# A two-block transformer kernel whose program order comes from another timing model

## The chip, the cores and the metric

The kernel runs on one core of one Trainium2 chip. The metric is the device time of one execution in microseconds (us). The kernel before took a median of 1812.11 us over three runs, from 1811.02 to 1816.88.

## The reference, cut to what matters

256 tokens of 1024 features pass through a first block of two layers and then a second block of two layers. All arithmetic is float32.

A layer of the first block projects the tokens with one wide matrix and runs three attention-like branches: retention (4 heads in chunks of 128 tokens), sliding-window attention (6 heads) and latent attention (6 heads, keys and values expanded from a normalised latent). Their outputs are joined, projected and added to the scaled input, and a layer norm follows. Then a router picks for every token the best of 4 groups and two of the 4 experts in it, and 16 experts (gate and up projection, SiLU, down projection) are applied:

```python
mix = jnp.concatenate([ret_o, swa_o, mla_o], axis=-1) @ w_out[l]
x = layer_norm(DEEPNORM_ALPHA * x + mix, ln1_g[l], ln1_b[l])
ffn = grouped_moe(x, router_w, router_bias, exp_w_gate_up[l], exp_w_down[l])
x = layer_norm(DEEPNORM_ALPHA * x + ffn, ln2_g[l], ln2_b[l])
```

A layer of the second block is a feed-forward network with 2816 inner features, a mixer (windowed attention with 8 heads, pooling over four widths, and sigmoid gates on both branches) and a second such feed-forward network, each behind an RMS norm.

## The kernel before

**Weights.** All weights lie in DRAM in the order of use. `Weights.fill` (line 335) loads the next tile of up to 2048 columns by 128 rows on SyncE's queue into one of six buffers. `Weights._run` (line 342) takes the tiles apart into pieces of at most 1024 columns and splits each into two parts whose sum is the weight: ScalarE casts the high part (`whi`, line 358), and VectorE, or GpSimd for pieces listed by hand in `POOL_STEPS`, subtracts to get the low part (`wlo`, line 360). Five pieces can be open at a time:

```python
nc.scalar.copy(hi[:, :n], r[:, c : c + n])
engine = nc.gpsimd if (p is t[-1] and name == "dn") or self.step in self.pool_steps() else nc.vector
ins = engine.tensor_tensor(
    out=lo[:, :n], in0=r[:, c : c + n], in1=hi[:, :n].bitcast(F32), op=ALU.subtract
)
```

The activations are split in the same way, and every large product is three products (high by high, high by low, low by high), all issued from line 425.

**Stages.** `attention1` (line 647) makes the projections of the latents (`oq`, `okv`), retention's queries and keys (`orq`), values (`ov`), the expanded latents (`oqr`, `ouq`, `ouk`, `omv`), then latent attention through `attend` (line 770), the sliding-window projection (`osq`), retention (`og`, `scr`, `oret`), sliding-window attention and the output projection (`oo`). In `attend` the scores of a head (`sc`) go through `softmax_head` (line 600) on VectorE and ScalarE, are transposed (`pt`) and multiplied with the values (`po`). `moe` (line 1008) does the norm, the router (`lg`, `cn`), gathers the tokens by group (`og`) and runs the 16 experts (`ogu`, `yg`, `ya`). `ffn` (line 1266) runs 22 steps of 128 inner features (`u`, `v`, then the down projection `f` of the step before). At its head `rms_T` (line 532) transposes the tokens (`trx`, line 527), splits them (`xT`, lines 510 and 511) and takes the reciprocal root of the mean square (lines 492 to 501). `mixer` (line 1312) does queries and keys (`oq`), values (`ovp`), attention, pooling (`opl`), gates (`ogt`), branches (`obr`) and the output projection (`oz`), and ends with the sum `hmx` (line 1441):

```python
for t in range(2):
    for n in range(2):
        c = slice(n * 512, (n + 1) * 512)
        V.tensor_tensor(out=hn[:, t, c], in0=h[:, t, c], in1=oo[t][n], op=ALU.add)
```

**What sets the order.** The code names the engine of every instruction, but not its place in that engine's queue. When the `TileContext` of `kernel` (line 1542) closes, a scheduler makes the order. It walks through the program on a timing model of the machine. Whenever an engine of the model can take an instruction, it gets the one that stands first in the program among those whose inputs and buffers are ready in the model. The order found is the order in which each engine's queue runs on the chip, in which a waiting instruction holds up what stands behind it. So a weight split of a later stage can go ahead of an attention step that is not ready. The program has two runtime branches (one in each layer's `moe`), and no instruction is moved across them. A few orders are fixed by hand with `tc.issue_after` and one with `tc.high_priority`; dummy products (`keep_clock`, line 433) stand at four places (lines 924, 969, 1183 and 1447).

Of the kernel before, what the change touches and what calls it, by code (L numbers as in the profile page):

```python
# [17 lines left out]
PSUM = bass.MemoryType.PSUM  # L18
# [29 lines left out]
# ---------------------------------------------------------------------------  # L48
# The order in which the weights are consumed: (array, layer, row, column, width).
# None closes the current DMA tile.  # L50
# ---------------------------------------------------------------------------
# [61 lines left out]
def layout():  # L113
    """Packs the recipe into pieces of at most PIECE columns and DMA tiles of at most RAW."""
# [36 lines left out]
def pack_weights(a):  # L151
    """Lays the weight matrices out in the order of use."""
# [53 lines left out]
# per-partition parameter columns  # L206
# [10 lines left out]
# parameters replicated over the partitions  # L217
# [9 lines left out]
# token-major vectors, one row each  # L227
# [25 lines left out]
# ---------------------------------------------------------------------------  # L253
# Constants that depend on shapes alone.
# ---------------------------------------------------------------------------
# [69 lines left out]
class Weights:  # L325
    """The stream of weights: DMA tiles, each piece split exactly into two float32r parts."""
# [8 lines left out]
    def fill(self):  # L335
        """Loads the next DMA tile."""
        off, w, t = self.tiles.pop(0)
        r = self.raw.tile([P, RAW], F32, name="raw", tag="raw")
        self.nc.sync.dma_start(out=r[:, :w], in_=self.flat[off : off + w * P].rearrange("(p c) -> p c", p=P))
        self.loaded.append((r, t))  # L340
# [40 lines left out]
def build(ctx: ExitStack, tc: tile.TileContext, ap, tap=None, parts=("b1", "b2")):  # L381
# [41 lines left out]
    # -- small pieces of arithmetic -------------------------------------------------  # L423
# [3 lines left out]
    def mm3(out, a, b, start, stop):  # L427
        """out += a^T b for operands split as (high, low)."""
        mm(out, a[0], b[0], start, False)
        mm(out, a[0], b[1], False, False)  # L430
        mm(out, a[1], b[0], False, stop)

    def keep_clock(n):
        """Products of zeros that nobody reads: the tensor engine halves its clock when it idles."""
# [4 lines left out]
    def gemm_wide(name, x, nk, outs, order=None, nseg=1, tail=1):  # L439
        """Tokens on the partitions: outs[t] is a list of (bank columns, segment columns).  # L440
        The first token tile finishes its last `tail` steps before the second starts them."""
# [11 lines left out]
    def gemm_block(name, x, nk, out):  # L453
        """Features on the partitions, all tokens along the columns."""
# [4 lines left out]
    def gemm_halves(name, x, nk, out):  # L459
        """The same with x = [high | low] along the columns: the result is the sum of out's halves."""  # L460
# [5 lines left out]
    def rsqrt_n(x, r, n, factor):  # L466
        """r = factor / sqrt(x) for [P, n] of positive values."""
# [17 lines left out]
    def rsqrt(x, name, factor=1.0):  # L485
        """factor/sqrt of a [P, 1] column of positive values."""
# [17 lines left out]
    def split_evac(hi, lo, src, scale=None):  # L504
        """hi + lo = src * scale, src in PSUM."""
# [13 lines left out]
    def transpose_scaled(xn, hl, gain):  # L519
        """hl = split of (token-major xn)^T * gain, gain per feature."""  # L520
# [11 lines left out]
    def rms_T(h, gain, name, work, hl=None):  # L532
        """Splits (h * gain)^T; the tokens' factors 1/rms follow where they commute with the
        products: as a column for each token tile and as a row on every partition."""
# [21 lines left out]
    def ln_stats(r, t, name):  # L556
        """Mean and 1/sqrt(var + eps) of the tokens of tile t."""
# [9 lines left out]
    def ln_hat(r, name):  # L567
        """(r - mean) / sqrt(var + eps), token-major."""
# [11 lines left out]
    def affine_T(xh, hl, g, b, work):  # L580
        """hl = split of xh^T * g + b."""
# [18 lines left out]
    def softmax_head(work, sc, width, masks, scales, nsink, sink, name):  # L600
        """sc: PSUM scores of two query tiles side by side, widths given. Returns normalised
        probabilities. scales are the negated factors of the scores."""
# [31 lines left out]
    def swap_halves(src, dst):  # L634
        """Swaps the 32 lower with the 32 upper features of every 64."""
# [3 lines left out]
    def rope(src, swapped, dst, cosT, sinT):  # L639
        """dst = src * cos + swapped * sin."""  # L640
# [5 lines left out]
    # -- block 1 -------------------------------------------------------------------  # L646
    def attention1(l, x, hl, work, cb):
        """x token-major, hl its split transpose. Returns what turns a token tile of x into alpha*x + mix,
        and the router's weights."""
# [10 lines left out]
        # latent projections, tokens on partitions  # L660
# [38 lines left out]
        # transposes of the latents  # L699
        ct = work.tile([P, 2, 5, T], F32R, name="ct", tag="ct")  # L700
        cth, ctl = ct[:, 0], ct[:, 1]
        # per head: 64 features without positions, then the rotated halves of its pair of heads,
        # those of the other head zero in the keys
# [14 lines left out]
        # retention's queries and keys, and the values  # L718
# [15 lines left out]
        # expanded latents  # L734
# [35 lines left out]
        def attend(name, score, vals, masks, scales, sinks, nsinks, first):  # L770
            """Six heads of causal attention, two to each 128-feature block of mix from the given one on.
            The scores of a head are computed ahead of the softmax of the one before."""
# [24 lines left out]
        # latent attention  # L797
# [11 lines left out]
        # sliding-window projections  # L809
# [8 lines left out]
        # retention  # L818
# [3 lines left out]
        for t in range(2):  # L822
            # g * (1 + tanh(g/2)) * gn; the half follows with the group norm
# [45 lines left out]
        # sliding-window attention  # L869
# [10 lines left out]
        # output projection and residual  # L880
# [14 lines left out]
    def router_weights(l, work):  # L895
        """The router's weights with the gain of the norm before it taken in, each expert's made
        to sum to 0 over the features (so that they see no mean), and its product with the bias."""
# [648 lines left out]
```

## Time and profile before

| | before |
|---|---|
| median of three runs | 1812.11 us |
| span of the profiled execution | 1808.4 us |
| own time of the profiled execution | not given beside its span |
| instructions | 24789 |
| TensorE busy | 1686.0 us (93%) |
| weight loads of TensorE busy | 1420.2 us (79%) |
| VectorE busy | 1248.8 us (69%) |
| ScalarE busy | 984.5 us (54%) |
| GpSimd busy | 316.4 us (17%) |
| mean granted TensorE clock | 0.969 |

The profile is of one execution. PE is TensorE's products, PEld its weight loads, DVE VectorE, ACT ScalarE, POOL GpSimd and SP SyncE. The span runs from the first instruction to the last; a run's time also holds what lies around it. A busy share is an average over all stages, so the stages are looked at one by one.

### The profile page before, as it was taken

How to read it: one execution, taken by the hardware profiler on the slowest of the kernel's cores; microseconds unless marked ns; L12 is line 12 of the kernel's file. 1: busy time of each engine (PE TensorE's matmuls, PEld its weight loads, DVE VectorE, ACT ScalarE, POOL GpSimd, SP SyncE). 2: the span in 40 equal slices, each digit the busy share in tenths (PEclk: the TensorE clock that was granted, in tenths of full speed). 3: DMA queues.
4: the chain of work that ended last, by engine and by line, in shares of the span. 5: the costliest groups of instructions: out<-in, count | busy, mean ns of one | idle time of the engine just before them, and what ended most of it. 6: DMA issues, size and time to landing. Idle time of an engine off the chain costs nothing.

```text
span 1808.4 us, 24789 instructions
## 1 busy us (share of the span) xinstructions
PE 1686.0 (93%) x9258; PEld 1420.2 (79%) x9258; DVE 1248.8 (69%) x2161; ACT 984.5 (54%) x1641; POOL 316.4 (17%) x161
## 2 busy tenths in 40 slices
PE   9897988899889897999899989998999999989997
PEld 8776766788667676888798978887888787968886
DVE  6668788775778878666675576666666666666665
ACT  5644766564456674555555455555555456445553
POOL 2204243512223334000300220003000210130000
PEclk9998999999989999999999989998999999989999
DMA  9332778552148775555352535553555433445540
GB/s 371 135 117 94 285 296 298 210 208 97 70 176 311 303 282 196 207 186 186 135 178 97 194 140 187 186 186 130 196 186 186 163 129 123 172 149 201 187 163 24
DMA packets 49422, 331.86 MB, mean 184 GB/s; under 512 B 5648, under 2 KB 5904, under 8 KB 13712
## 3 DMA queue, kind: packets, MB, share of 16 engines
q1 hardware_dynamic: 47952, 325.73, 49.9%
q10 hardware_dynamic: 1344, 4.49, 0.9%
q8 instruction: 75, 1.23, 0.3%
q14 instruction: 51, 0.42, 0.1%
HBM read 326.79 MB, written 1.05 MB: 181 GB/s over the span
## 4 chain that ended last, share of the span: by engine, by line
PE 60%; DVE 7%; ACT 2%; issue 1%; ACTq 0%; DVEq 0%
PE u L425 13%; PE f L425 13%; PE v L425 12%; PE ogt L425 5%; PE ogu L425 4%; PE obr L425 3%; DVE wlo L360 2%; PE oz L425 2%; PE ovp L425 2%; PE oq L425 2%; ACT whi L358 2%; PE sc L425 1%; PE po L425 1%; DVE fhp L1293 1%; PE opl L425 1%
## 5 line engine op out<-in xcount | busy, mean ns | idle before, releaser
L358 ACT CAST whi<-raw 128x1024 fp32r<-128x1024 f32 (+2 forms) x611 | 629.9, 1033 | 561.7 <-PE v L425 114.7
L360 DVE TENSOR_TENSOR wlo<-raw,whi 128x1024 fp32r<-128x1024 f32 (+5 forms) x512 | 655.8, 1292 | 327.9 <-ACT whi L358 324.7
L360 POOL TENSOR_TENSOR wlo<-raw,whi 128x1024 fp32r<-128x1024 f32 (+4 forms) x99 | 229.5, 2327 | 919.1 <-ACT whi L358 890.8
L425 PE MATMUL f<-whi,fhh 128*128 128x512 f32 x704 | 235.4, 396 | 9.3 <-ACT fhh L1298 8.6
L425 PE MATMUL u<-xT_f,whi 128*128 128x512 f32 x528 | 194.4, 407 | 4.0 <-DVE xT_f L511 4.0
L425 PE MATMUL v<-xT_f,whi 128*128 128x512 f32 x528 | 190.0, 399 | 0.0
L425 PEld LDWEIGHTS f<-whi,fhh 128*128 128x128 f32 x704 | 133.0, 190 | 43.3 <-ACT fhh L1298 10.4
L425 PE MATMUL u<-xT_f,wlo 128*128 128x256 f32 x528 | 150.2, 284 | 0.0
L425 PE MATMUL v<-xT_f,wlo 128*128 128x256 f32 x528 | 148.3, 281 | 0.0
L425 PE MATMUL f<-wlo,fhh 128*128 128x512 f32 x352 | 139.2, 396 | 0.0
L425 PE MATMUL ogu<-wlo,xgh 128*128 128x512 f32 x256 | 105.7, 413 | 24.1 <-DVE wlo L360 24.0
L425 PEld LDWEIGHTS u<-xT_f,whi 128*128 128x128 f32 x528 | 101.8, 193 | 29.1 <-DVE xT_f L511 5.1
L425 PEld LDWEIGHTS v<-xT_f,whi 128*128 128x128 f32 x528 | 99.2, 188 | 24.5
L425 PE MATMUL ogu<-whi,xgl 128*128 128x512 f32 x256 | 101.8, 399 | 5.6 <-DVE xgl L598 5.5
L425 PE MATMUL ogu<-whi,xgh 128*128 128x512 f32 x256 | 104.6, 408 | 0.0
L425 PEld LDWEIGHTS u<-xT_f,wlo 128*128 128x128 f32 x528 | 102.1, 193 | 2.3
L425 PEld LDWEIGHTS v<-xT_f,wlo 128*128 128x128 f32 x528 | 99.8, 189 | 0.0
L425 PE MATMUL ogt<-xT_mx,whi 128*128 128x256 f32 x512 | 97.4, 287 | 0.0
L425 PEld LDWEIGHTS ogu<-wlo,xgh 128*128 128x128 f32 x256 | 49.0, 192 | 47.6 <-DVE wlo L360 39.4
L425 PE MATMUL yg<-whi,hh 128*128 128x512 f32 x256 | 84.6, 391 | 1.2 <-ACT hh L507 1.2
L425 PEld LDWEIGHTS ogt<-xT_mx,whi 128*128 128x128 f32 x512 | 80.4, 191 | 3.0 <-issue 1.5
L425 PEld LDWEIGHTS f<-wlo,fhh 128*128 128x128 f32 x352 | 66.8, 190 | 10.7
(555 smaller groups left out, 3275.7 us busy)
## 6 DMA issues: line engine op xcount, KB each, us to landing
raw<-in_wflat_dram SPq DMA_DIRECT2D x276, 1024.0 KB, 4.8
raw<-in_wflat_dram SPq DMA_DIRECT2D x10, 960.0 KB, 5.6
gb<-in_rows_dram SPq DMA_DIRECT2D x8, 512.0 KB, 4.8
raw<-in_wflat_dram SPq DMA_DIRECT2D x4, 992.0 KB, 4.7
raw<-in_wflat_dram SPq DMA_DIRECT2D x4, 512.0 KB, 3.8
raw<-in_wflat_dram SPq DMA_DIRECT2D x2, 1008.0 KB, 7.0
raw<-in_wflat_dram SPq DMA_DIRECT2D x2, 976.0 KB, 7.8
raw<-in_wflat_dram SPq DMA_DIRECT2D x4, 384.0 KB, 6.4
```

The source lines that it names most:

```text
L358: nc.scalar.copy(hi[:, :n], r[:, c : c + n])
L360: ins = engine.tensor_tensor(out=lo[:, :n], in0=r[:, c : c + n], in1=hi[:, :n].bitcast(F32), op=ALU.subtract)
L425: return TE.matmul(out, lhsT=lhsT, rhs=rhs, start=start, stop=stop)
L1293: V.tensor_tensor(out=hp, in0=row, in1=hp, op=ALU.mult)
```

## The change

The program's order is made with the scheduler's timeline model instead of its default one. The library describes the timeline model as a simulator of how long each device is occupied, and as the more detailed of its two timing models. Nothing else in the program differs: the same instructions with the same operands, engines, buffers and hand-written orders. The diff also removes comments and docstrings throughout, each line of which stays as a blank line, so line numbers are the same. Of the many hunks that only do that, one stands here:

```diff
@@ -333,7 +333,7 @@
         self.segs = self._run()
 
     def fill(self):
-        """Loads the next DMA tile."""
+
         off, w, t = self.tiles.pop(0)
...
@@ -1539,7 +1539,7 @@
         arrays[f"in_{name}_dram"] = v
         ap[name] = nc.dram_tensor(f"in_{name}_dram", v.shape, mybir.dt.from_np(v.dtype), kind="ExternalInput").ap()
     ap["out"] = nc.dram_tensor("out_0_dram", (T, D), F32, kind="ExternalOutput").ap()
-    with tile.TileContext(nc) as tc:
+    with tile.TileContext(nc, schedule_with_timeline_sim=True) as tc:
         build(tc, ap)
     r = run_bass_kernel_spmd(nc, [arrays], core_ids=[0])
     return r.results[0]["out_0_dram"].reshape(1, T, D)
```

## Rows read from the trace of the kernel before

**Rows 1.** The page, span and busy time of each engine.

```profile
span 1808.4 us, 24789 instructions
...
PE 1686.0 (93%) x9258; PEld 1420.2 (79%) x9258; DVE 1248.8 (69%) x2161; ACT 984.5 (54%) x1641; POOL 316.4 (17%) x161
```

**Rows 2.** The page, the span in 40 slices, in tenths.

```profile
PE   9897988899889897999899989998999999989997
...
PEclk9998999999989999999999989998999999989999
```

**Rows 3.** Stage windows: length, busy us (instructions) by engine, clock, DMA share, GB/s.

```profile
26.00:136.00 110.00, 102.81 (x644) 87.12 (x643) 72.10 (x229) 60.25 (x134) 17.15 (x11) 0.98 0.47 172
368.00:480.00 112.00, 105.11 (x650) 88.78 (x649) 70.77 (x232) 61.01 (x134) 16.77 (x11) 0.97 0.37 130
136.00:187.00 51.00, 40.99 (x207) 32.28 (x206) 41.37 (x91) 24.56 (x35) 19.85 (x11) 0.80 0.29 100
480.00:532.00 52.00, 39.52 (x201) 31.78 (x200) 40.58 (x88) 24.11 (x34) 19.23 (x11) 0.80 0.27 95
187.00:338.00 151.00, 138.12 (x594) 105.94 (x593) 119.54 (x110) 104.00 (x127) 56.07 (x24) 1.00 0.78 286
532.00:683.00 151.00, 138.22 (x595) 105.97 (x594) 119.33 (x110) 105.13 (x127) 56.44 (x22) 1.00 0.76 288
...
1069.00:1240.00 171.00, 170.89 (x894) 145.15 (x893) 114.62 (x163) 88.36 (x144) 4.83 (x3) 1.00 0.53 186
```

**Rows 4.** Windows of the seven joints between stages: the mixer's, and their sum.

```profile
1040.00:1066.00 26.00, 19.00 (x88) 15.78 (x87) 18.25 (x36) 11.44 (x23) 9.70 (x5) 0.80 0.24 83
...
sum 185.00, PE 141.24 PEld 120.00 DVE 140.02 ACT 86.48 POOL 74.64; mean PE 20.18 PEld 17.14 DVE 20.00 ACT 12.35 POOL 10.66
```

**Rows 5.** TensorE's waits: total us, times, longest us.

```profile
PE ogu L425 <- DVE wlo L360: 24.0, 35, 1.7
PE trx L527 <- DVE hmx L1441: 13.0, 2, 6.5
PE cn L425 <- DVE rGb L957: 9.0, 2, 5.4
PE f L425 <- ACT fhh L1298: 8.6, 3, 2.9
PE u L425 <- DVE x2hl L598: 6.2, 1, 6.2
...
PE ouk L425 <- DVE wlo L360: 5.3, 1, 5.3
```

**Rows 6.** The page, groups of the weight split: busy us, mean ns, idle before.

```profile
L358 ACT CAST whi<-raw 128x1024 fp32r<-128x1024 f32 (+2 forms) x611 | 629.9, 1033 | 561.7 <-PE v L425 114.7
L360 DVE TENSOR_TENSOR wlo<-raw,whi 128x1024 fp32r<-128x1024 f32 (+5 forms) x512 | 655.8, 1292 | 327.9 <-ACT whi L358 324.7
```

**Rows 7.** The page, weight loads: KB each, median us from issue to landing.

```profile
raw<-in_wflat_dram SPq DMA_DIRECT2D x276, 1024.0 KB, 4.8
```

**Rows 8.** Windows after each layer's last head, output projection `oo` on TensorE alone.

```profile
128.40:136.30 7.90, 7.88 (x34) 1.00 0.33 133
...
471.60:479.60 8.00, 7.91 (x34) 1.00 0.37 131
```

**Rows 9.** Timeline of VectorE at the first mixer's end: start us, us, instruction.

```profile
1040.21 1.37 DVE L1441 TENSOR_TENSOR hmx<-h,oz 128x512 f32<-128x512 f32 x2 [6.53 <-PE oz L425]
...
1043.33 0.16 DVE L497 SCALAR_TENSOR_TENSOR f20y<-f20a,f20y 128x1 f32<-128x1 f32 x1
1043.52 2.31 DVE L498 SCALAR_TENSOR_TENSOR f20a<-f20y,ms_f 128x1 f32<-128x1 f32 x1
...
1048.16 2.26 DVE L500 SCALAR_TENSOR_TENSOR f20a<-f20y,f20y 128x1 f32<-128x1 f32 x1
...
1050.91 1.27 DVE L1441 TENSOR_TENSOR hmx<-h,oz 128x512 f32<-128x512 f32 x2
```

**Rows 10.** Timeline of GpSimd in the same stretch.

```profile
1043.42 6.98 POOL L360 TENSOR_TENSOR wlo<-raw,whi 128x1024 fp32r<-128x1024 f32 x3 [3.10 <-ACT whi L358]
```

## The prediction

> **What bounds the kernel now.** I read the page's busy table first: TensorE is busy for 1686.0 us of a span of 1808.4 us, VectorE for 1248.8, ScalarE for 984.5, GpSimd for 316.4 [rows 1]. So at most 1808.4 - 1686.0 = 122 us are idle time of the bounding engine, and the rest is matrix products that no order makes fewer. The slices show where the idle time is: TensorE's digits are 8 or 9 nearly throughout, and the granted clock is at 8 tenths or more in every slice [rows 2]. Then I cut the span into stages, with the same landmarks in both layers [rows 3]. In a feed-forward body TensorE is busy for 170.89 of 171 us. In the experts it is 138.1 of 151 in both layers, in attention 102.8 of 110 and 105.1 of 112, in the router and gather 41.0 of 51 and 39.5 of 52 at a mean clock of 0.80. The seven joints between stages, 185 us together, hold 141.24 us of TensorE work, so 44 us idle [rows 4]. Last, TensorE's own waits name who is late: the experts' products wait 24.0 us for VectorE's weight split, the transposes after the mixers 13.0 us for `hmx`, the rank counts 9.0, the feed-forward tail 8.6 for `fhh`, the first product of block 2 6.2, `ouk` 5.3 [rows 5].
>
> **The change, part by part.** No instruction is added, removed or resized. The flag alone acts; the deleted comments and docstrings leave blank lines and emit nothing, so that edit costs 0. The scheduler walks the program on a timing model and gives an engine that is free the ready instruction that stands first in the program. With the flag that model is the library's more detailed one, so other moments count as "free" and "ready", and some instructions change places in the queues of TensorE, VectorE, ScalarE, GpSimd and SyncE. What each move can cost depends on what covers it:
>
> *Feed-forward bodies* (four, some 700 us): TensorE never idles [rows 3], so what moves on the other queues is hidden by the products in front of it. Cost 0. If the cover went, one split late by its own 1.29 us [rows 6] in each of 88 steps would be 114 us; with VectorE busy 114.62 of 171 us there [rows 3] I take 0.
>
> *SyncE's queue*: 276 loads of 1 MB land in a median 4.8 us [rows 7]. A feed-forward step uses three pieces of 1024 columns, one and a half loads, and six load tiles are open, four steps ahead. A load moved by one or two places is hidden; if that cover is gone it costs at most its 4.8 us. I take 0.
>
> *Attention*: the softmax chain of a head is short pieces on four engines, and TensorE fills the gaps with the projection that follows it in the program. When the last head ends, 34 of the output projection's products are still to do, 7.88 us in one layer and 7.91 in the other [rows 8]. A chain that gets up to 7.9 us longer costs 0, since TensorE does that work earlier; what goes beyond is paid in full. I take 0.
>
> *Experts*: two layers have two separately made orders of the same code, and they took the same 151 us with 138.12 and 138.22 busy [rows 3]. That is the nearest thing to a second order that the trace has. I take 0. The ends are -24.0 (all waits for the split gone [rows 5]) and one split of 1.29 us more per expert, less the wait of 24.0 / 32 = 0.75 that is there already: 32 x 0.54 = +17.
>
> *Joints, router, start of attention*: 7 joints, 2 routers, 2 stretches of expanded latents, so 11 places where a chain of small VectorE and ScalarE operations is alone on the path. After the mixer VectorE does `hmx` for tile 0, the reciprocal root for tile 0, then `hmx` for tile 1, and only then can TensorE transpose [rows 9]. A step of such a chain that becomes ready just after its engine was given a weight split waits for it: 1.29 us on VectorE, 1.03 on ScalarE [rows 6]. A more detailed model has more parts in each step, so I expect it to see such a chain arrive later and hand out more splits in between. No row shows how often. The ends are none and one at each place, 0 to 11 x 1.29 = +14.2; below zero is possible too and is the second rival. I take half, **+7.1 us**, because the gaps of both kinds occur here: the mixers' joint has no split on VectorE in its chain [rows 9], while `ouk` waits 5.3 us for splits that stand behind other VectorE work [rows 5].
>
> The sum is 0 + 0 + 0 + 0 + 0 + 7.1, so a span of 1815.5 from 1808.4. The profile gives no other time of its own execution; the median of the runs, 1812.11, lies 3.7 above the span, and I take that as what lies around it: **1819 us**. A measurement of this kernel can tell about 0.3%, 5.4 us, from no change: under 1806.7 is faster, over 1817.5 slower.
>
> **The rivals.**
>
> *No effect that can be measured.* The queues change places only where the products cover it, as the two layers' 151 us suggest; the attention windows' idle 7.2 and 6.9 us agree as well [rows 3]. Against it: the joints' 44 us of idle time [rows 4] leave something to move. 1812 us.
>
> *Faster: the joints get shorter.* At the mixers' joint three VectorE operations on one column per partition take 2.31 (the first) to 2.26 us (the last), where the one before them takes 0.16 [rows 9], while GpSimd runs three subtracts back to back from 1043.42 for 6.98 us [rows 10]. The second `hmx` stands behind them and TensorE waits 6.5 us, twice in the program [rows 5]. If the new order puts the three operations after `hmx`, or GpSimd's subtracts elsewhere, the wait shrinks to about the 1.27 us of `hmx` [rows 9]: 2 x (6.5 - 1.3) = -10.4. The stretch around it has a mean clock of 0.80 [rows 4], so 40% of 26 us at 1.2 GHz where 2.4 is the other level, 5.2 us of lost work each; if that went too, up to -10.4 more. From half of the wait for `x2hl`, -3.1 [rows 5]. Together -13.5 to -23.9; I take -17: 1795 us. Against it: both layers have this same wait, so it comes from something steady in how the chain becomes ready. The Trainium skill, "SBUF — State Buffer", section "Who interferes with whom", states that a VectorE operation with two SBUF inputs is fully blocked by a GpSimd operation that reads SBUF; the trace agrees, 2.31 against 0.16 us, and by that rule a model without this lock would not know to avoid it, which speaks against this rival.
>
> The Trainium skill, "Perfetto Trace Analysis", section "Identifying the Most-Contended Engine", says that matmul busy time does not measure the room that is left, and that the weight loads' busy share does. By it the room would be 1808.4 - 1420.2 = 388 us [rows 1] instead of 122, and a tenth of it won would give 1773 us. The bodies speak against it: TensorE's products leave a gap of 0.11 us in 171 there [rows 3], so the extra room is inside the products' own pacing. I give it 2 of this rival's 32 in 100.
>
> *Much slower: TensorE is committed too early.* If the new model lets an engine take work further ahead of its end, ready projection products and splits are put before the softmax chain's own pieces. Place: the four attentions of block 1, with six heads each. Price: one VectorE split and one ScalarE cast more per head, 1.29 + 1.03 = 2.3 us, 6 x 2.3 = 13.9 us per attention, of which the 7.9 us of output projection cover a part [rows 8]: 4 x 6 = +24. With one split more per expert, +17 (above), 1853 us. It decides from the point where a chain is lengthened by more than 7.9 us. For it: the fill lasts to the end of each attention with not much to spare. Against: VectorE is busy for only 72.10 of 110 us there [rows 3].
>
> **How the numbers follow.** Slightly slower, the forecast at 1819: 36 in 100 (its own range 1817.5 to 1828). No effect: 23. Faster: 32. Much slower: 9. So faster 0.32, same 0.23, slower 0.36 + 0.09 = 0.45. The range reaches into the faster case to 1788 (-24, its full price) and into the slow one to 1846, leaving out some 8 in 100 below and 5 above.
>
> **What would show it.** Right: the same instruction counts; feed-forward bodies as long as now; TensorE's idle time in the joints up by some 7 us, its waits naming splits on VectorE or casts on ScalarE. The first rival: all stages within 2 us. The second: the waits for `hmx` gone or short, and the three stretched operations back at 0.16 us. The third: TensorE idle at the end of the attentions, no output projection left after the last head. I would be wrong in kind if a feed-forward body grew or shrank, since I count those at nothing, or if loads came late.

## The result and the profile after

The changed kernel takes 1827.42 us in the median of seven runs (1823.8 to 1836.75); the kernel before, timed beside it, 1814.62 (1811.02 to 1820.39, seven runs). The ratio is 1.0077 with a 95% interval of 1.0057 to 1.0098, so it is slower by 0.8%. The profiled execution took 1825.92 us at a span of 1824.1, so 1.8 us lie around the span; against the span of before that is 15.7 us more. Executions of one order differ by up to 13 us, the longer ones at a lower mean clock (1810.42 us at 0.973 and 1823.54 at 0.963 in `b2_timeline` below), and the landmarks of two executions of the default order by up to 2.6 us, so a smaller difference between two single executions says little by itself.

First, the page of the changed kernel: span, busy times, TensorE's slices and granted clock, the groups of the weight split and the loads.

```profile
span 1824.1 us, 24806 instructions
...
PE 1693.2 (93%) x9258; PEld 1424.3 (78%) x9258; DVE 1250.9 (69%) x2161; ACT 983.7 (54%) x1643; POOL 331.5 (18%) x161
...
PE   8987988898979897999899989998999999989997
...
PEclk9998999999879998999999999999999999989999
...
L360 DVE TENSOR_TENSOR wlo<-raw,whi 128x1024 fp32r<-128x1024 f32 (+5 forms) x512 | 673.6, 1327 | 309.3 <-ACT whi L358 305.1
...
raw<-in_wflat_dram SPq DMA_DIRECT2D x276, 1024.0 KB, 4.8
```

The same products and vector operations run; ScalarE has two instructions more (see the end of this section). TensorE idles for 1824.1 - 1693.2 = 130.9 us against 122.4 [rows 1], 8.5 more, and its same 9258 products are busy for 7.2 us longer. Most of that is the clock: laid over the trace's clock records, 89.8 us of the busy time pass at 1.2 GHz against 79.4, which is 5.2 of the 7.2 us. The loads land as they did [rows 7]. On VectorE the split takes 1327 ns in the mean against 1292 [rows 6]. From one execution to the next the busy part scatters more than the idle part: the control run below, whose order is that of the kernel before, has 121.3 idle and 1689.7 busy, 85.6 of it at 1.2 GHz. So part of the 7.2 us is scatter.

Where the time goes can be read from products that both traces have. The table gives the end of the last product of a kind, or the start of the first `yg`, in us from the span's start. The last column is the loss up to there; what a stage loses is the difference of two rows.

| landmark | before | after | after - before |
|---|---|---|---|
| output projection `oo`, first layer | 136.28 | 140.84 | 4.56 |
| rank counts `cn` | 149.91 | 151.21 | 1.29 |
| first `yg` of the experts | 186.89 | 191.76 | 4.87 |
| last `ya` | 337.90 | 346.33 | 8.43 |
| `oo`, second layer | 479.51 | 484.95 | 5.44 |
| `cn` | 493.15 | 495.33 | 2.18 |
| first `yg` | 531.98 | 540.91 | 8.93 |
| last `ya` | 682.90 | 696.28 | 13.37 |
| first feed-forward, last `f` | 890.51 | 905.37 | 14.86 |
| first mixer, last `oz` | 1044.93 | 1061.87 | 16.94 |
| second feed-forward, last `f` | 1247.70 | 1260.85 | 13.14 |
| third feed-forward, last `f` | 1445.95 | 1458.55 | 12.60 |
| second mixer, last `oz` | 1599.10 | 1615.07 | 15.97 |
| last `f` | 1796.79 | 1810.97 | 14.17 |
| end | 1808.41 | 1824.10 | 15.69 |

Block 1 loses 13.4 us: 4.6 in the first attention, 3.6 and 6.8 from `cn` to the first `yg`, 3.6 and 4.4 in the experts, with gains of 3 us at each `cn` and over the joint and attention of the second layer. Block 2 loses 2.3: the two mixers 2.1 and 3.4, the feed-forward networks after them gain 3.8 and 1.8. The mixers' loss is no scatter: in the eight kernels with this order of block 2 the first mixer takes 156.5 to 158.1 us, in the four with the default order 153.2 to 154.4.

TensorE's waits of the changed kernel, with the columns of [rows 5]:

```profile
PE ogu L425 <- DVE wlo L360: 27.8, 26, 1.7
PE og L425 <- DVE aff L597: 11.4, 2, 6.5
PE f L425 <- ACT fhh L1298: 8.6, 3, 2.9
PE trr L866 <- DVE ro L862: 7.7, 2, 3.9
PE trx L527 <- DVE hmx L1441: 7.3, 2, 3.6
PE u L425 <- DVE x2hl L598: 5.6, 1, 5.6
```

The waits for `cn` (9.0) and `ouk` (5.3) have left the list and that for `hmx` went from 13.0 to 7.3. In their place TensorE waits 11.4 us for the gather's affine steps and 7.7 for the retention's group norm.

Then windows of the changed kernel, as in [rows 3, 4, 8]: the second feed-forward body of the first layer, the mixer's joint, the stretches from the group norm to the end of both attentions, and what is left at the end of the first. The last fence has the first attention's stretch in the kernel before.

```profile
1082.00:1253.00 171.00, 171.00 (x897) 145.77 (x897) 115.57 (x165) 89.82 (x147) 4.82 (x2) 1.00 0.54 192
...
1057.00:1083.00 26.00, 20.76 (x107) 17.62 (x106) 18.81 (x38) 14.49 (x26) 9.66 (x5) 0.87 0.26 84
...
107.00:141.00 34.00, 29.02 (x126) 19.49 (x125) 14.53 (x50) 14.92 (x38) 0.00 (x0) 0.90 0.24 81
450.50:485.00 34.50, 29.50 (x123) 20.12 (x122) 14.15 (x49) 14.48 (x38) 0.00 (x0) 0.85 0.22 82
...
137.00:141.00 4.00, 3.44 (x16) 2.35 (x15) 1.22 (x3) 0.49 (x2) 0.00 (x0) 1.00 0.62 155
```

```profile
110.50:136.30 25.80, 24.51 (x117) 17.07 (x117) 14.73 (x55) 13.98 (x35) 0.00 (x0) 1.00 0.33 123
```

The body is as full as before. The joint holds 1.8 us more TensorE work in 26 us. The attentions have a new loss: in 34 us after the group norm TensorE idles for 5 us and its clock is 0.90 and 0.85, so 34 x 0.10 x 2 = 6.8 and 34.5 x 0.15 x 2 = 10.3 us pass at 1.2 GHz, where the kernel before idles for 1.3 us and has the full clock. After the last head 12 products of `oo` are left (in a window of 16 instructions, 3.44 us) where there were 34 in 7.88 [rows 8]; between `trr` and the last `po` stand 48 of them instead of 26.

What that does to the softmax chain shows in the transposes `pt` (L789) of the first layer's sliding-window heads. First before, then after: the instructions with their number and duration, first and last start, and who waited for them.

```profile
L789 PE MATMUL pt<-cperm,pr_s x18: 270/272/329, 111.4 to 126.6; 128*128 128x128 f32 x18
...
  ACT ptS L791: 3.3, 3
  DVE pr_s L611: 1.6, 3
```

```profile
L789 PE MATMUL pt<-cperm,pr_s x18: 271/273/369, 112.3 to 135.6; 128*128 128x128 f32 x18
...
  ACT ptS L791: 12.0, 4
  DVE pr_s L611: 8.8, 4
```

The six heads start 0.9 us later and end 9.0 us later, and ScalarE and VectorE now wait 12.0 and 8.8 us for TensorE. VectorE's own queue has room: after the first head VectorE stands idle for 4.34 us until `pt`, while TensorE runs eight `oo` products, most of them at half clock.

A correction: the section on the kernel before says that no instruction is moved across the two runtime branches. The listings of the two programs, which give every engine's instructions in the order of its queue, show that this is not so. In each layer 15 `ogu` products, a load, a split with its cast and a SiLU stand ahead of the branch (L1109) in the default order and behind it in the timeline's. By the same listings the two orders differ by moving at least 1136 of 9238 instructions on TensorE, 450 of 2003 on VectorE, 322 of 1539 on ScalarE, 5 on GpSimd and 10 on SyncE.

With that SiLU, a load of ScalarE's function table moved too. In the kernel before one load, 1.28 us long, stands ahead of the branch in idle time; in the changed kernel there are two in each layer, 10 in the program against 8, and the second stands right ahead of the first SiLU, on which the first `yg` hangs. Before, then after:

```profile
171.20 1.28 ACT L1159 ACT_TABLE_LOAD   x1
174.77 0.38 ACT L1159 ACTIVATE sl<-ogu 128x256 f32<-128x256 f32 x1 [2.29 <-PE ogu L425]
```

```profile
186.44 1.28 ACT L1159 ACT_TABLE_LOAD   x1
187.73 0.38 ACT L1159 ACTIVATE sl<-ogu 128x256 f32<-128x256 f32 x1
```

It can account for at most 2 x 1.28 = 2.6 us of the loss between `cn` and `yg`; no run tests it by itself.

### The profile page after: what moved, and what is told of

Same layout as the page of the kernel before. It is cut to its first block, busy times and chain, and to the rows that moved or that the text cites. A ratio compares the mean times of both kernels' runs of the same rounds, so it can differ in the third digit from the quotient of the medians.

```text
span 1824.1 us, 24806 instructions
## 1 busy us (share of the span) xinstructions
PE 1693.2 (93%) x9258; PEld 1424.3 (78%) x9258; DVE 1250.9 (69%) x2161; ACT 983.7 (54%) x1643; POOL 331.5 (18%) x161
## 4 chain that ended last, share of the span: by engine, by line
PE 55%; DVE 4%; ACT 1%; issue 1%; ACTq 0%
PE u L425 14%; PE f L425 13%; PE v L425 13%; PE ogt L425 5%; PE obr L425 2%; PE oz L425 2%; PE ovp L425 2%; PE oq L425 2%; PE sc L425 1%; ACT whi L358 1%; PE po L425 1%; DVE fhp L1293 0%; PE trx L527 0%; PE pt L1381 0%; DVE wlo L360 0%
## 5 line engine op out<-in xcount | busy, mean ns | idle before, releaser
L360 DVE TENSOR_TENSOR wlo<-raw,whi 128x1024 fp32r<-128x1024 f32 (+5 forms) x512 | 673.6, 1327 | 309.3 <-ACT whi L358 305.1
L425 PE MATMUL ogu<-wlo,xgh 128*128 128x512 f32 x256 | 107.0, 419 | 29.2 <-DVE wlo L360 27.8
L425 PEld LDWEIGHTS f<-wlo,fhh 128*128 128x128 f32 x352 | 67.7, 192 | 11.8
```

Of the source, the lines that this page charges most:

```text
L360: ins = engine.tensor_tensor(out=lo[:, :n], in0=r[:, c : c + n], in1=hi[:, :n].bitcast(F32), op=ALU.subtract)
L425: return TE.matmul(out, lhsT=lhsT, rhs=rhs, start=start, stop=stop)
```

## Experiments

Twelve kernels. In several, `tie` adds issue-order edges (no waits) between consecutive instructions of each engine's queue in a chosen set, so that they keep the order that the other scheduler gave them; the rest of the program is left to the scheduler named, which makes its order anew beside them.

```diff
+def tie(tc):
...
+            if prev is not None:
+                tc.add_manual_dep(
+                    i, prev, mybir.DependencyInfo(mybir.DependencyClass.NoSync, mybir.DependencyReason.DATA), reason="tie"
+                )
...
+            tie(tc)
             with tc.If(most > P):
```

All results, with the kernel before as timed in the same comparison (us; idle is the span less TensorE's busy time, of one execution):

| run | median | before | ratio, 95% interval | span | TensorE busy | idle |
|---|---|---|---|---|---|---|
| kernel before | | | | 1808.4 | 1686.0 | 122.4 |
| changed kernel | 1827.42 | 1814.62 | 1.0077 (1.0057 to 1.0098) | 1824.1 | 1693.2 | 130.9 |
| all_default | 1813.97 | 1811.88 | 1.0008 (0.9995 to 1.0022) | 1811.0 | 1689.7 | 121.3 |
| exp_default | 1823.64 | 1813.56 | 1.0056 (1.0035 to 1.0076) | 1824.5 | 1695.4 | 129.1 |
| att_default | 1825.53 | 1813.56 | 1.0073 (1.0047 to 1.0100) | 1823.4 | 1688.8 | 134.6 |
| b2_default | 1822.78 | 1813.56 | 1.0076 (1.0049 to 1.0104) | 1820.4 | 1686.2 | 134.2 |
| b2_timeline | 1819.33 | 1811.81 | 1.0031 (1.0014 to 1.0049) | 1818.6 | 1694.0 | 124.6 |
| pe_default | 1842.59 | 1813.56 | 1.0166 (1.0136 to 1.0196) | 1840.0 | 1698.6 | 141.4 |
| others_default | 1900.06 | 1811.48 | 1.0486 (1.0455 to 1.0516) | 1898.1 | 1724.3 | 173.8 |
| dummies_last | 1829.39 | 1811.48 | 1.0082 (1.0050 to 1.0114) | 1827.6 | 1693.8 | 133.8 |
| gates_last | 1831.84 | 1811.48 | 1.0115 (1.0083 to 1.0146) | 1828.0 | 1692.2 | 135.8 |
| norm_first | 1827.44 | 1811.48 | 1.0081 (1.0051 to 1.0111) | 1829.7 | 1696.6 | 133.1 |
| warm_trr | 1826.50 | 1811.81 | 1.0075 (1.0053 to 1.0097) | 1825.7 | 1693.9 | 131.8 |
| sums_first | 1805.98 | 1811.81 | 0.9959 (0.9943 to 0.9974) | 1804.8 | 1689.4 | 115.4 |

**The control.** The timeline model with everything tied to the default order.

> The control for the runs with ties: the timeline model is asked for, and every instruction of every engine is tied to the default order. If the order is all that the change does, and if ties cost nothing by themselves, it runs like the kernel before: within 2 us of its median in this comparison. If the ties (or what the model settles beside the order) cost time, it is slower by several us, and the 1842.6 and 1900.1 us of the runs with one engine's order from each scheduler say less than they seem to.

The ratio is 1.0008 and its interval holds 1: no difference that can be told, though the medians lie 2.1 us apart. The change acts through the order alone, and ties cost at most 0.2% by themselves.

**One part of the program at a time.** Three kernels with the timeline's order, in which one part keeps the default order, and one with the two halves the other way round.

> The timeline's order everywhere but in the two MoE blocks (from the norm's transposes over router, gather and sixteen experts to the residual): there the instructions of each engine are tied to each other in the order that the default scheduler gave them. By the ends of the stages in the two traces the changed kernel loses 3.9 us in the first MoE block and 7.9 us in the second, of its 15.7. Theory A, that the new order costs time where it stands (work of no hurry placed ahead of a chain's step, here the dummy products ahead of the last two ya products and the splits around the gather): 11.8 us come back, 1827.4 to about 1815.6 us, and the waits og<-aff (4.9 and 6.5 us) are gone. Theory B, that the loss is only moved (what the MoE blocks lose, the stages before and after have gained by the same instructions): under 4 us come back, over 1823.

Theory A misses. By the medians 3.8 us came back, not 11.8, which is theory B's range, and the interval (1.0035 to 1.0076) overlaps that of the changed kernel. The experts are back at 151.4 and 151.8 us from the first `yg` to the last `ya` (151.0 and 150.9 in the kernel before, 154.6 and 155.4 in the changed one), so their loss does lie in their order. The waits `og<-aff` are gone as foreseen, but another takes their place at the seam: TensorE waits for the norm's root between the transposes of tile 0 and tile 1, and the step from `oo` to `lg` takes 7.7 us more than in the kernel before (13.1 against 5.4). The waits of this run at the norm and the gather:

```profile
PE og L457 <- DVE pm L1087: 7.6, 4, 2.0
...
PE trx L1076 <- DVE ln10r L533: 6.3, 2, 3.1
```

> The timeline's order everywhere but in the opening, the two attention blocks of block 1 and the joint between the layers, which are tied to the default order. By the ends of the stages the opening gains 5.8 us up to the retention's gates and the rest of the first attention loses 10.4, the joint and the second attention gain 3.0: together the changed kernel loses 1.6 us here. Theory A (costs stand where they show): 1827.4 to about 1825.8, within 2 us of it; the wait of TensorE for the group norm's transposes trr (3.8 us in each layer) goes, the wait for ouk's copies (5.3 us) comes back. Theory B (the gain of the opening is paid for in the attention, and the MoE's loss was prepared here by splits and loads in another order): 4 us or more away from 1825.8, in either direction.

The median is the one expected, but not for its reason. Both named waits moved as said (`trr` 1.4, `ouk` 5.4), and the end of the first attention is 3.4 us earlier than in the changed kernel; but the joint and the second attention take 5.1 us longer. The MoE blocks are of another shape too, with a shorter gather (no wait for affine steps) and 22.7 us of waits for `cn`:

```profile
PE cn L467 <- DVE rGb L999: 22.7, 2, 12.6
...
PE ouk L467 <- DVE wlo L360: 5.4, 1, 5.4
```

> The timeline's order in block 1 as in the changed kernel, and all of block 2 (four feed-forward blocks, two mixers, the end) tied to the default order. By the ends of the stages block 2 loses 2.3 us. The prediction had put its loss here (late splits in the joints, 7.1 us with the router's two). Theory A: 1827.4 to about 1825.1. The prediction's theory (late splits in the joints): 3 to 5 us come back, 1822.4 to 1824.4. A gain of the new order here would show as a time over 1828: the hmx waits, 6.5 us in each mixer's end under the default order, come back and outweigh the mixers' opening.

By the medians 4.6 us came back, by the ratio nothing; the two intervals cover both. Its `hmx` waits are 13.0 us again, the mixers take as long as in the kernel before, and its span is 3.7 us under that of the changed kernel.

> The default order in block 1, and block 2 tied to the timeline's order: the counterpart of the run with block 2 in the default order (1822.8 us, 4.6 under the changed kernel). If the two halves are independent, block 2 costs here what it gave there, by the ends of the stages 2.3 to 3.7 us and by the medians 4.6: 1817 to 1819. If the loss sits in the fit of the halves, 1814 to 1815 or over 1822. The feed-forward blocks gain 4 us (hmx waits of 3.6 in place of 6.5 us) and the mixers lose 5.4 in either case.

The ratio gives 0.0031 x 1811.8 = 5.6 us of loss (2.5 to 8.9), which fits the independent halves and does not exclude the other theory. So block 2's order costs some 3 to 6 us as a best estimate, and block 1's the rest, some 8 to 11. In block 2 TensorE's idle time is up by only 2.2 us (124.6 against 122.4); the busy part is up by 8.0.

**One engine's order from each scheduler.**

> TensorE's instructions are tied to the default order in the whole program; VectorE, ScalarE, GpSimd and SyncE take the order that the timeline model gives beside it. Theory A1, that the loss lies in TensorE's own order (products issued ahead of earlier ones: 1383 against 736 in the last block): nearly all of it comes back, 1813 to 1817. Theory A2, that it lies in VectorE's (three splits between the steps of the group norm's root, the split between the gather's affine steps): TensorE waits longer at fixed places, less than half comes back, 1820 or more.

> The counterpart of the run with TensorE's default order (1842.6 us): VectorE, ScalarE, GpSimd and SyncE are tied to the default order in the whole program, and TensorE's order is left to the timeline model beside it. Theory A2, that the loss lies in the order of VectorE and ScalarE: it goes, 1812 to 1817. Theory A1, that it lies in TensorE's: 1822 or more. Theory A3, that an order on one engine fits only the order on the others that it was made with: this run loses too, though less than the 29 us of its counterpart, 1817 to 1835, with waits of TensorE at places where neither kernel has them.

Neither A1 nor A2: nothing came back in either run. TensorE in the default order, with the others left to the timeline model, costs 1.7%, and the reverse 4.9%, both more than the change itself; idle time rises to 141.4 and 173.8 us. A3 holds in kind, but its size is far off: the reverse loses 88.6 us, not less than 29. TensorE waits in new places, in others_default for the retention's scores and the mixer's gates:

```profile
PE trr L919 <- DVE ro L915: 9.9, 2, 4.9
...
PE oret L478 <- DVE sT L891: 8.2, 4, 4.3
PE ogt L478 <- DVE gt L1464: 7.5, 4, 1.9
```

But the free engines did not take the changed kernel's order. By the listings, TensorE's order in others_default is 799 moves from the changed kernel's and 1051 from the default one, where those two are 1166 apart; VectorE's in pe_default is 277 and 327 moves from them, which are 450 apart. So these runs show that a new order made beside fixed queues of another scheduler is worse than either scheduler's own. They do not show on which engine the 0.8% lies.

**Repairs of single places in the changed kernel.** One more edge makes the model set its order anew: by the listings dummies_last is 4 moves from the changed kernel on TensorE and 4 on VectorE, gates_last 107 and 100, norm_first 68 and 34. So only the first moves one place alone.

```diff
-            keep_clock(WARM[2])
+            with tc.issue_after(tail.ins):
+                keep_clock(WARM[2])
```

> The changed kernel with one tie more in each MoE block: the 60 dummy products at its end stand behind the last ya product on TensorE (in the changed kernel 18 of them stand ahead of the last two). Nothing else moves. Theory A (ready work of no hurry placed ahead of a chain's last step costs its own time there): the stretch from the first yg to the last ya shrinks by the 18 products, some 2 us in each layer, and the end falls by about 4 us, 1827.4 to 1823. Rival: the products fill a wait that is there anyway (the split of the last y on VectorE), so the last ya stands where it stood and the end moves by less than 1 us.

The end did not fall, as the rival has it, though the last `ya` did move: from the first `yg` to it is 2.0 and 1.9 us shorter, and from it to the first transpose of the norm 1.9 and 2.5 us longer. In the first layer, from VectorE's last split of `y` to that transpose it is 8.0 us in the kernel before, 8.3 in the changed one and 8.3 here: the chain of sums and norm on VectorE sets that time, not the last two `ya`. So some 4 us of the loss that the table puts at the last `ya` are no loss.

```diff
-            gates = late()
+            with tc.issue_after(gathered.ins):
+                gates = late()
```

> The changed kernel with the chain of the gates (L981 to L1003, which needs only the router's scores) put behind the last affine step of the gather on VectorE. In the changed kernel its steps, with two splits of 2.2 us among them, stand ahead of all affine steps, and the first of these starts at 167.26, 11.1 us after the first og product, against 2.9 us in the kernel before (157.53 after 154.63); TensorE waits 4.9 and 6.5 us for it. Theory A: the og<-aff waits go, and the stretch from the counts to the first yg falls by 3 to 5 us in the first layer and 5 to 7 in the second: the end falls by 8 to 12 us, to 1815 to 1819. Rival: the gates are late then, gp waits for them as it did in the kernel before (1.9 to 2.1 us), and the branch behind: under 4 us in all.

The rival holds; the time is 4 us above the changed kernel's, with intervals that overlap. `og<-aff` falls from 11.4 to 6.7 us and `gp`, which needs the gates, rises from 2.4 to 9.0:

```profile
PE gp L425 <- issue: 9.0, 2, 4.8
...
PE og L425 <- DVE aff L597: 6.7, 2, 3.4
```

Half of the affine steps' lateness stays, and the changed kernel's timeline shows why. GpSimd, then VectorE:

```profile
150.95 5.19 POOL L1032 TENSOR_TENSOR xs<-x,xs 128x512 fp32r<-128x512 f32 x4 [53.91 <-DVE rGb L957]
156.11 8.28 POOL L360 TENSOR_TENSOR wlo<-raw,whi 128x1024 fp32r<-128x1024 f32 x3
```

```profile
156.35 2.33 DVE L992 TENSOR_TENSOR rgt<-rvb 128x16 f32<-128x16 f32 x1
158.61 0.26 DVE L987 TENSOR_REDUCE rvs<-rpk 128x4 f32<-128x16 f32 x2
158.79 2.23 DVE L993 TENSOR_TENSOR req<-rvb 128x16 f32<-128x16 f32 x1
160.94 4.53 DVE L360 TENSOR_TENSOR wlo<-raw,whi 128x1024 fp32r<-128x1024 f32 x2
165.40 0.16 DVE L992 TENSOR_TENSOR rgt<-rvb 128x16 f32<-128x16 f32 x1
```

The steps with two inputs that fall beside GpSimd's three subtracts take 2.2 to 2.3 us here, whatever their size: `rgt` 0.16 alone, a split 1.22. In the kernel before, GpSimd's run stretches from 141.36 to 154.19, beside the router's chain, where `rgs` and `rGb` take 1.2 to 2.1 us each; TensorE's wait for `cn` [rows 5] is there. In the changed one it stretches from 150.95 to 164.39, behind `cn` and beside the gather. It starts later, as the order of the rows suggests, because tile 0 is no longer ahead of tile 1. In the kernel before, its share of the 34 last `oo` products ended early and its norm was done when the last product ended (root `ln10r` at 136.54, last `oo` at 136.28). In the changed kernel, with 12 left, the sums of both tiles run in one row after 140.20 and both norms side by side behind them (`ln10r` at 146.89, last `oo` at 140.84).

```diff
-        gemm_wide(
-            "wo", ...
+        with tc.issue_after(normed.ins):
+            gemm_wide(
+                "wo", ...
```

> The changed kernel with VectorE's splits of the output projection's weights put behind the last step of the retention's group norm (three of them, 1.22 us each, stand between the last steps of its root in the changed kernel). Theory A: ro is ready some 3.5 us earlier, the wait trr<-ro (3.8 and 3.9 us) and the half clock behind it (6.8 and 10.2 us at half rate, worth 3.4 to 5) go, and the stretch to the last oo falls by 4 to 8 us in each layer: 1812 to 1820. Rival: TensorE has no other work left there, since it was issued earlier, and what the norm gains the output projection loses to its splits, which are now later (oo waits for wlo): under 3 us in all.

The rival holds. TensorE reaches `trr` 4.5 us earlier, and its waits for it are still 2.9 and 3.3 us: with the splits, `oo` products went behind the norm that had filled the time (16 stand ahead of `trr` instead of 36). The last head's transposes stand at 135.9 us, as in the changed kernel (135.6).

```diff
         tr = bank("tr", "trr")
+        warm = [mm(tr[:, :256], zeros[:, :P], zeros, True, True) for _ in range(28)]
```

> The changed kernel with 28 dummy products (about 0.12 us each, 3.3 us) in each attention in front of the transposes trr, where TensorE waits 3.8 and 3.9 us for the group norm; they write zeros that the transposes overwrite. Theory: the wait costs twice, once as idle time and once through the half clock that follows it (6.8 and 10.2 us at half rate, 3.4 and 5.1 us); with the products the wait stays and the half clock goes: 1827.4 to about 1819. Rival: the half clock falls a little later instead, or has another cause: within 2 us of 1827.4.

The dummy products, which compute nothing of the result, did at their place what the theory says of the clock: the wait for `trr` falls to 0.7 us in all, and the clock between 100 and 140 us is full, as it is from 450 to 490 in the second layer. The first attention is 2.3 us shorter than in the changed kernel, the second with its joint 1.9. But four other runs have this attention's order without the dummies (exp_default, b2_default, dummies_last, gates_last): all fall to half clock at the wait for `trr`, in the first layer for 3 to 10 us, and the first attention ends at 138.4 to 141.0 us there, here at 138.6. So at most 2.4 us are won at that place. The window of the first, then that of dummies_last and gates_last:

```profile
100.00:140.00 40.00, 37.80 (x196) 27.26 (x195) 21.85 (x84) 19.21 (x49) 0.00 (x0) 1.00 0.22 79
```

```profile
100.00:140.00 40.00, 35.02 (x165) 24.80 (x165) 22.14 (x84) 19.22 (x50) 0.00 (x0) 0.96 0.21 79
```

```profile
100.00:140.00 40.00, 35.11 (x148) 24.83 (x148) 19.51 (x80) 17.61 (x47) 0.00 (x0) 0.87 0.18 63
```

The two MoE blocks behind them take 4.4 and 2.7 us longer than in the changed kernel, which is near the scatter (the first is 3.2 us longer in b2_default as well, in the same order), and the end stays within the rival's 2 us.

**The wait that both orders share.** The default order, with the mixer's sums ahead of the root.

```diff
-        rs = [rms_scale(h, t, name) for t in range(2)]
+        if name == "f2":
+            with tc.issue_after(summed[-1].ins):
+                rs = [rms_scale(h, t, name) for t in range(2)]
+        else:
+            rs = [rms_scale(h, t, name) for t in range(2)]
```

> The default order with one tie more: in the norm behind each mixer VectorE takes the four sums hmx first and the steps of the root behind them (in the kernel before the last two sums stand behind the first root, whose steps take 2.26 to 2.31 us beside a split on GpSimd instead of 0.15 to 0.22; TensorE's transposes wait 6.5 us for them, twice, and 10.2 us at half clock follow, twice). Theory H, that the wait is a matter of the place in VectorE's queue: it shrinks to the two sums behind the last oz product, 1.3 us, which gives 5.2 us in each layer; with the half clock gone too (10.2 us at half rate cost 5.1) up to 10.3: 1814.6 to between 1794 and 1804. Rival: the root's slow steps now stand ahead of the splits xT_f, and u waits for those instead: less than 4 us in all, over 1810.

1805.98 us, 0.9959 (0.9943 to 0.9974): faster than both kernels. Its size lies between the two theories' (over 1804, under 1810). VectorE at the first mixer's end, to be read beside [rows 9]:

```profile
1043.26 1.37 DVE L1447 TENSOR_TENSOR hmx<-h,oz 128x512 f32<-128x512 f32 x2 [6.53 <-PE oz L425]
1047.34 1.37 DVE L1447 TENSOR_TENSOR hmx<-h,oz 128x512 f32<-128x512 f32 x2 [2.71 <-PE oz L425]
...
1049.24 1.95 DVE L496 SCALAR_TENSOR_TENSOR f20a<-f20y,ms_f 128x1 f32<-128x1 f32 x1
1051.12 0.86 DVE L511 SCALAR_TENSOR_TENSOR xT_f<-trx,cols,xT_f 128x256 fp32r<-128x256 f32 x2
```

The last two sums now follow the last `oz` at once, and the 6.5 us wait is gone. Half of it comes back where the rival said: `u` and the later transposes wait 2.7 and 1.9 us for `xT_f`, which stands behind a stretched step of the root (over the program, waits for `xT_f` rise by 7.3 us where those for `hmx` fall by 13.0). TensorE's idle time is 7.0 us less over the program, and 5.8 us of time are won.

## Why the prediction was right, and where it was wrong

The forecast was slower by a little, 1819 us in 1788 to 1846; measured were 1827.4. The sign and the range hold. The sum's +7.1 us stand against 12.8 by the medians and 15.7 by the spans. But the term that carried the sum is not where the time went, and the range also held a faster kernel and an unchanged one: the sign was in good part luck. The 3.7 us added for what lies around the span were too many; it is 1.7 to 2.6 us in the executions listed with their spans.

*Feed-forward bodies and SyncE, 0 each:* right. TensorE is busy for 171.00 of 171 us against 170.89 [rows 3], the loads land in 4.8 us, and no wait of TensorE names a load.

*Joints, router and start of attention, +7.1 by late splits:* half right. The joints behind block 2's mixers got shorter, not longer, and so did the stretch to `cn`; the wait at `ouk` is gone. The waits that this term and its rival speak of (`hmx`, `cn`, `x2hl`, `ouk`, with `trr` and `og<-aff` as the new ones) are 13.0 + 9.0 + 6.2 + 5.3 + 1.5 = 35.0 us before and 7.3 + 5.6 + 7.7 + 11.4 = 32.0 after. The chains with splits in between do occur (three between the last steps of the group norm's root, two ahead of the gather's affine steps), but the waits cleared elsewhere are as large. What failed is the step "11 places, half of one split each", since it took the chains of the kernel before as undisturbed and added to them alone.

*Attention, 0 by a cover of 7.9 us:* the reasoning failed, the size less. "TensorE does that work earlier" was taken to cost nothing. Done earlier, it stood in front of the next head's transposes, so TensorE became what the softmax chain waits for (12.0 us on ScalarE against 3.3). The cover was used up: 12 products after the last head instead of 34. And with the cover went the head start of tile 0's norm, which moved GpSimd's subtracts from the router to the gather; that link is read from the rows and no run tests it alone. The stretch from the retention's gates to the end of `oo` is 10.4 us longer in the first layer and 10.0 in the second, whose heads wait as well (14.6 us on ScalarE). But 18 products of the latent attention that stood ahead of the gates now stand behind them, and what lies ahead is 5.8 and 13.0 us shorter. Net, the first attention loses 4.6 us and the second with its joint gains 3.0. A gap in front of the chain also cost twice here, since the products behind it ran at 1.2 GHz for a while (clock 0.90 and 0.85).

*A term that is missing:* the sum counts idle time alone. By the trace 5.2 of the 15.7 us are products at half clock, part of it scatter.

*Experts, 0:* short by some 4 us. The wait of `ogu` for splits went from 24.0 to 27.8 us, and exp_default's default order there gives the experts' time back. The argument, two layers with the same 151 us, showed only that one scheduler makes much the same order twice.

*The rivals.* "No effect" is excluded by the interval. "Faster: the joints get shorter" happened in part: 5.7 of its 10.4 us at `hmx`, by the very move it names (one sum went ahead of the last stretched root step), and sums_first gives 5.8 us when nothing else changes. At the router `rgt` takes 2.33 us beside GpSimd's subtract and 0.16 without, so what is moved beside GpSimd matters more here than how long it is. The Trainium skill, "SBUF — State Buffer", section "Who interferes with whom", says that a VectorE operation with two SBUF inputs contends with a GpSimd operation that reads SBUF; the trace agrees. "TensorE is committed too early" is the mechanism that the attentions show, at a smaller price than its +24: net 4.6 us in the first attention and -3.0 in the second with its joint. That price also took the 7.9 us of cover off each of four attentions, where the output projection closes only two. The far end of 1773 us has nothing in the runs for it.

*What stays open.* Of the 15.7 us, 8.5 are idle time of TensorE and 7.2 longer products. No repair that was tried gives either back: where one shrank a wait, or the dummy products did, no gain at the end could be told from scatter. So why block 1 loses its 8 to 11 us is argued from the stages, not shown by a run. Whether several repairs together would win it was not tried, nor was sums_first in the timeline's order. What the timeline model gets wrong about the chip cannot be read from these runs; the control shows only that nothing but its order matters.

## What to carry to other kernels

An order of instructions is one plan for all queues: fixing some engines in one scheduler's order and leaving the others to another's model cost up to 4.9% here, and a repaired wait mostly moved to the next step. So judge an order by its time over several executions, with TensorE's idle time and landmarks beside it, not by one wait that went away. Work that fills gaps is not free to move forward: once it is spent, the chain behind it stands bare. A landmark can move as well as the work, so add up all stages before one of them is blamed. Where the profile shows an operation that TensorE needs waiting in a queue behind steps of another chain, put it first by hand: that gave 0.4% in the default order.

## What the runs showed of the hardware that was not expected

VectorE steps of 128x16 elements and splits of 128x1024 took nearly the same 2.23 to 2.33 us beside GpSimd's subtracts (0.16 and 1.22 alone), so a short step loses most there. And 28 dummy products of zeros in each wait, about 3 us of work, kept the clock full for the rest of both attentions (1.00 from 100 to 140 us and from 450 to 490), where the changed kernel and four more executions of that order without them show 0.87 to 0.96 and 0.86 to 0.87.
